# Two passes for three: one 512 column matmul for both parts of x in feed forwards, gates and down products

## The chip, the cores and the metric

One core of one Trainium2 chip runs the whole program. The metric is the device time of one execution in microseconds (us). Engines are named as in the profile: PE (TensorE) does matmuls into PSUM, PEld is its weight loads, DVE is VectorE, ACT is ScalarE, POOL is GpSimd, SP issues the DMAs of the weights.

## What is computed

Two transformer blocks of two layers each on 256 tokens of 1024 features, float32. Cut to what the change touches:

```python
def swiglu_ffn(h, w_up, w_down):                       # block one, twice a layer
    a, b = jnp.split(h @ w_up, 2, axis=-1)
    return (jax.nn.silu(a) * b) @ w_down
...
    x = x + 0.5 * swiglu_ffn(rmsnorm(x, ffn1_norm[l]), ffn1_w_up[l], ffn1_w_down[l])
    x = x + mixer(...)            # attention, conv; ends (g_attn * y_attn + g_conv * y_conv) @ w_out
    x = x + 0.5 * swiglu_ffn(rmsnorm(x, ffn2_norm[l]), ffn2_w_up[l], ffn2_w_down[l])
...
        up = dwconv_centred(h @ w_up[l], conv_w[l], conv_b[l])      # block two
        gate, val = up[..., :D_FF_2], up[..., D_FF_2:]
        x = x + (jax.nn.silu(gate) * val) @ w_down[l]
```

The feed forwards are 1024 -> 2 x 2816 -> 1024. The gates g_attn and g_conv are sigmoids of a 1024 -> 2 x 1024 product of the mixer's normed input.

## The kernel before

The residual stream x lies in SBUF as eight tiles of 128 features x 256 tokens. Each float32 product is made of float32r passes: an operand is split into a rounded part (h) and the rest (l), and W x = Wl xh + Wh xh + Wh xl. `mm3` (L326 to L332) issues these three passes, each 128x128 weights by 256 columns of tokens, into the same 256 columns of one PSUM bank. The weights are the stationary side.

The weights come as a stream of units of 128x1024 (some 128x768) values in the order of their use. `fetch` (L294) loads a unit into one of four raw buffers, `ahead` (L304) splits it: ScalarE copies the rounded part (wh, L312), VectorE subtracts (wl, L313). Splits run three units ahead of their use and loads six. Five buffers hold split units.

A feed forward (`ffn1` L467 in block one, `ffn2` L1141 in block two) has 22 up pairs and 8 down blocks. `up_pair` (L443) and `pair_half` (L432) take two units for 16 products of three passes: eight blocks of x, for the gate column block and the value column block side by side in one PSUM bank, 256 columns each. In block one `evac_up` (L474) then reads PSUM: VectorE t = pa * R (1/rms of the tokens, L476), ScalarE silu (L477), VectorE t * pb (L479), split into hh (ACT L338) and hl (DVE L339). 1/rms comes late: the products run on x * gain, the sum of squares is summed over partitions on TensorE after the first pair (`rms_cols`, L397) and spread to rows after the second (`rows`, L384), and the PSUM banks of the first pairs wait for it. In block two the first three pairs are treated so (L1159), and the later ones run on the normed x. There the evacuation is a conv of three taps (L1162 to L1164), silu and a product. `down` (L449) takes three units a block for 22 products into 256 columns of a bank. Its `evac` in block one is VectorE d = a * 0.5 * R (L497) and x + d (L498), in block two x + a (L1187). `operand` (L419) splits x * gain for the next stage into tiles xh and xl per block.

In block one's mixer the gates (`gate`, L806) are eight pairs like the up pairs. Their halves are laid between the heads of the attention by hand (L821 to L838). The result is multiplied by R on VectorE (L812, L813). The mixer's other products (`token_major`, L566) have x as the stationary side and the weights as 512 moving columns. Those of the conv (`conv_forward`, L661), of the attention's projection and of block two's mixer are outside the change but use its operands or its PSUM pool.

PSUM has two pools of four banks: `acc` (L246) gives a bank of 512 values from pool ps, `aux` (L249) one from pool px for scores, transposes and sums. The framework works out an order for each engine's instructions and the waits between engines from the program. A buffer is given out again when everything that used its tile is done. ScalarE's and VectorE's queues run in the order set then.

Of the kernel before, what the change touches and what calls it, by code (L numbers as in the profile page):

```python
# [27 lines left out]
P = 128  # L28
# [27 lines left out]
FIRST = {1: -5, 3: -4, 5: -3, 7: -2}  # L56
# buffers of the weight stream, and how many units its splits and its loads run ahead
# [70 lines left out]
def shape_tables():  # L128
# [29 lines left out]
    # cosines at the frequencies 0..128, sines at 1..127: the rest follows by symmetry  # L158
# [35 lines left out]
# ----------------------------------------------------------------------------------------------  # L194
class Kernel:
    def __init__(self, ctx, tc, aps):
# [14 lines left out]
        self.ps = pool("ps", 4, space=bass.MemoryType.PSUM)  # L211
# [19 lines left out]
        self.rawq, self.splq = {}, {}  # L231

# [13 lines left out]
    def acc(self, s="acc"):  # L246
        return self.ps.tile([P, 512], F32, tag="acc", name=self.nm(s))
# [69 lines left out]
    def unit(self, n):  # L317
        """Rounded part and rest of the next unit of the stream."""
# [7 lines left out]
    def mm3(self, out, wh, wl, xh, xl, start, stop, skip=False):  # L326
        """out += W^T x, stationary W"""
# [6 lines left out]
    def split(self, src, hi, lo, scale=None):  # L334
        """hi = rounded src * scale, lo = the rest"""
# [16 lines left out]
    def square_sum(self, blocks, scales=None):  # L352
        """Sum over blocks of (block * scale)^2, elementwise on [128, 256]"""
# [14 lines left out]
    def mean_rows(self, sacc, count, eps):  # L368
        """Every partition: mean over features + eps, [128, 256]"""
# [7 lines left out]
    def rows(self, r):  # L377
        """[128, 2] with tokens on partitions -> [128, 256], the same row on every partition"""
# [13 lines left out]
    def mean_cols(self, sacc, count, eps):  # L392
        """The same with tokens on partitions, [128, 2]"""
# [13 lines left out]
    def exp_table(self):  # L407
        """ScalarE's table of exp, ahead of the attention"""
# [3 lines left out]
    def combine_v(self, v1, vg):  # L412
        """(v1 * v2)^-1/2 with v2 = vg / v1 + eps, that is (vg + eps * v1)^-1/2"""
# [5 lines left out]
    def operand(self, srcs, gains, b0=0):  # L419
        hs, ls = [], []  # L420
        for b, x in enumerate(srcs, b0):
            h = self.op.tile([P, S], F32R, tag=f"xh{b}", name=self.nm("xh"))
            lo = self.op.tile([P, S], F32R, tag=f"xl{b}", name=self.nm("xl"))
            hv, lv = (h, lo) if len(x.shape) == 2 else (h.rearrange("p (j r) -> p j r", r=4),
                                                        lo.rearrange("p (j r) -> p j r", r=4))
            self.split(x, hv, lv, gains[b - b0])
            hs.append(h)
            ls.append(lo)
        return hs, ls

# [1 line left out]
    def pair_half(self, a, o, half):  # L432
        xh, xl = o
# [3 lines left out]
        for kk in range(4):  # L437
            k = half * 4 + kk
            for ab in range(2):
                self.mm3(a[:, ab * 256:(ab + 1) * 256], wh[:, kk, ab], wl[:, kk, ab], xh[k], xl[k],  # L440
                         k == 0 and ab == 0, k == KB - 1, skip=True)

    def up_pair(self, o):  # L443
        a = self.acc()
        for half in range(2):
            self.pair_half(a, o, half)
        return a[:, :256], a[:, 256:]

    def down(self, h, evac):  # L449
        for ob in range(KB):  # L450
            a = self.acc()
            for k0, k1 in DOWN:
                wh, wl = self.unit((k1 - k0) * P)
                for k in range(k0, k1):
                    c = slice((k - k0) * P, (k - k0 + 1) * P)
                    hh, hl = h[k]
# [3 lines left out]
    def h_slots(self):  # L460
        tiles = []
        for i in range(0, NF, 4):
            hi, lo = self.t4("hh", F32R), self.t4("hl", F32R)
            tiles += [(hi[:, j], lo[:, j]) for j in range(min(4, NF - i))]
        return tiles

    def ffn1(self, x, o, late, meanwhile=()):  # L467
        """x += 0.5 * swiglu(x_normed); the norm's 1/rms is applied to the products.  late: pieces to run after
        the first pairs, each with the result of the one before; the last one gives 1/rms"""
        nc = self.nc  # L470
        h = self.h_slots()
        R = None

        def evac_up(n, pa, pb):  # L474
            t = self.t1("t")
            nc.vector.tensor_tensor(t, pa, R, op=ALU.mult)  # L476
            nc.scalar.activation(t, t, AF.Silu)  # L477
            f = self.t1("f")
            nc.vector.tensor_tensor(f, t, pb, op=ALU.mult)  # L479
            self.split(f, *h[n])  # L480

        got, pend = None, []
        for n in range(NF):
            pend.append((n, *self.up_pair(o)))
# [820 lines left out]
```

## Time and profile before

| | |
|---|---|
| runs shown (3) | 1998.09, 2011.82, 2012.04 us; median 2011.82 |
| profiled execution, span from the first to the last instruction | 1994.0 us |
| mean granted clock of TensorE | 0.996 |
| TensorE matmuls | 14760, busy 1972.2 us |
| VectorE / ScalarE | busy 1393.5 / 1121.9 us |
| read from HBM | 335.65 MB, 169 GB/s over the span |

The profile gives the span of the profiled execution and no time of its own around it: of the runs shown the lowest is 4.1 us above the span, the median 17.8 us. A matmul's row shows when it started and how long until its last result was there. Since matmuls overlap, the distance between the starts of two is what one costs in a stream. PE's granted clock is given as a share of 2.4 GHz. A row of the timeline ends with the engine's idle time before the instruction and what ended it.

### The profile page before, as it was taken

The numbers are of one execution on the slowest core, as the hardware profiler recorded it, in microseconds if no ns is written. First come the engines' busy times: TensorE is split into PE (matmuls) and PEld (weight loads), VectorE is DVE, ScalarE is ACT, GpSimd is POOL, SyncE is SP. The second block draws the span as 40 slices with busy tenths as digits, with TensorE's granted clock in tenths as the row PEclk, the third lists the DMA queues.
The fourth block names the chain that finished last, engine by engine and source line by source line (L and its number), as shares of the span: only waits on it lengthen the run. The fifth ranks groups of instructions, "written<-read, shape, count | busy, mean of one in ns | idle before, by whom it ended". The sixth has DMA issues, their size and how long they took to land. (4 is left out here: it accounts for less than half of the span.)

```text
span 1994.0 us, 37071 instructions
## 1 busy us (share of the span) xinstructions
PE 1972.2 (99%) x14760; PEld 1881.0 (94%) x14760; DVE 1393.5 (70%) x2364; ACT 1121.9 (56%) x2133; POOL 113.9 (6%) x111
## 2 busy tenths in 40 slices
PE   8999999999999999999999999999999999999999
PEld 8999878899999999998788999999889999899999
DVE  6765687857666576656877567666768985669973
ACT  5544555647544455445556575444676764577662
POOL 1000022100000000000212000000100000100000
PEclk9999999999999999999999999999999999999999
DMA  8655655434555555556545245556334655524654
GB/s 263 194 179 182 218 169 167 154 96 159 180 182 183 176 177 191 175 185 212 177 165 165 79 154 180 183 178 182 122 127 149 199 177 179 181 96 161 203 179 125
DMA packets 97260, 339.09 MB, mean 170 GB/s; under 512 B 11430, under 2 KB 13574, under 8 KB 96960
## 3 DMA queue, kind: packets, MB, share of 16 engines
q1 hardware_dynamic: 93024, 326.63, 50.5%
q0 software_dynamic: 2944, 8.11, 1.7%
q8 instruction: 115, 1.88, 0.4%
q10 hardware_dynamic: 1120, 2.00, 0.3%
q14 instruction: 57, 0.47, 0.1%
HBM read 335.65 MB, written 1.05 MB: 169 GB/s over the span
## 5 line engine op out<-in xcount | busy, mean ns | idle before, releaser
L313 DVE TENSOR_TENSOR wl<-raw,wh 128x1024 fp32r<-128x1024 f32 (+1 forms) x634 | 758.7, 1199 | 351.2 <-ACT wh L312 346.2
L312 ACT ACTIVATE wh<-raw 128x1024 fp32r<-128x1024 f32 (+1 forms) x634 | 655.3, 1037 | 582.8 <-PE acc L332 273.1
L330 PE MATMUL acc<-xh,wl 128*128 128x256 f32 x1760 | 502.8, 286 | 4.6 <-DVE wl L313 4.5
L331 PE MATMUL acc<-xh,wh 128*128 128x256 f32 x1760 | 499.7, 284 | 0.0
L332 PE MATMUL acc<-xl,wh 128*128 128x256 f32 x1760 | 498.5, 283 | 0.0
L330 PEld LDWEIGHTS acc<-xh,wl 128*128 128x128 f32 x1760 | 338.1, 192 | 6.3 <-DVE wl L313 5.3
L331 PEld LDWEIGHTS acc<-xh,wh 128*128 128x128 f32 x1760 | 338.2, 192 | 0.8
L332 PEld LDWEIGHTS acc<-xl,wh 128*128 128x128 f32 x1760 | 338.0, 192 | 0.0
L330 PE MATMUL acc<-hh,wl 128*128 128x256 f32 x1056 | 298.8, 283 | 0.0
L331 PE MATMUL acc<-hh,wh 128*128 128x256 f32 x1056 | 298.8, 283 | 0.0
L332 PE MATMUL acc<-hl,wh 128*128 128x256 f32 x1056 | 298.8, 283 | 0.0
L330 PEld LDWEIGHTS acc<-hh,wl 128*128 128x128 f32 x1056 | 202.8, 192 | 0.0
L331 PEld LDWEIGHTS acc<-hh,wh 128*128 128x128 f32 x1056 | 202.8, 192 | 0.0
L332 PEld LDWEIGHTS acc<-hl,wh 128*128 128x128 f32 x1056 | 202.8, 192 | 0.0
L578 PE MATMUL acc<-wl,xh 128*128 128x512 f32 x480 | 189.7, 395 | 0.5 <-DVE wl L313 0.5
L579 PE MATMUL acc<-wh,xh 128*128 128x512 f32 x480 | 187.9, 392 | 0.0
L580 PE MATMUL acc<-wh,xl 128*128 128x512 f32 x480 | 187.8, 392 | 0.0
L330 PE MATMUL acc<-xn,wl 128*128 128x256 f32 x608 | 172.1, 283 | 0.0
L331 PE MATMUL acc<-xn,wh 128*128 128x256 f32 x608 | 172.1, 283 | 0.0
L332 PE MATMUL acc<-xn,wh 128*128 128x256 f32 x608 | 172.1, 283 | 0.0
L330 PEld LDWEIGHTS acc<-xn,wl 128*128 128x128 f32 x608 | 116.7, 192 | 0.0
L331 PEld LDWEIGHTS acc<-xn,wh 128*128 128x128 f32 x608 | 116.7, 192 | 0.0
(278 smaller groups left out, 3072.3 us busy)
## 6 DMA issues: line engine op xcount, KB each, us to landing
raw<-wts SPq DMA_DIRECT2D x576, 512.0 KB, 3.4
raw<-wts SPq DMA_DIRECT2D x48, 384.0 KB, 3.1
brow<-b_in POOLq DMA_DIRECT2D x26, 256.0 KB, 3.8
raw<-dft SPq DMA_DIRECT2D x4, 512.0 KB, 3.5
tab<-tab ACTq DMA_DIRECT2D x1, 1024.0 KB, 8.1
out<-x SPq DMA_DIRECT2D x8, 128.0 KB, 3.5
raw<-dft SPq DMA_DIRECT2D x2, 384.0 KB, 3.4
wraw<-conv_w POOLq DMA_DIRECT2D x6, 124.0 KB, 4.9
```

Of the source, the lines that this page charges most:

```text
L312: nc.scalar.activation(h[:, :n], r[:, :n], AF.Copy)
L313: nc.vector.tensor_tensor(lo[:, :n], r[:, :n], h[:, :n].bitcast(F32), op=ALU.subtract)
L330: mm(out, wl, xh, start=start, stop=False, **k)
L331: mm(out, wh, xh, start=False, stop=False, **k)
L332: mm(out, wh, xl, start=False, stop=stop, **k)
L578: mm(accs[t], xh[k][:, ts], wl[:, c], start=k == 0, stop=False)
L579: mm(accs[t], xh[k][:, ts], wh[:, c], start=False, stop=False)
L580: mm(accs[t], xl[k][:, ts], wh[:, c], start=False, stop=k == KB - 1)
```

## The change

The rounded part and the rest of each operand come to lie side by side in one tile of 2 x 256 columns (`operand`, and `pairs` for the hidden layer and the others). A new `mm2` issues two passes: Wh with all 512 columns, so that the left half of a bank collects Wh xh and the right half Wh xl, and Wl with xh into the right half. Whoever reads the result adds the halves. Up pairs and gates therefore take two banks each (gate columns in one, value columns in the other), and pool ps becomes two tiles of two banks. `acc` hands out the two banks of a tile one after the other. `mm2` is used in block one's up pairs, its gates, and in all down products. Block two's up pairs and all other products keep `mm3` and the single bank (`whole=True`). In block one `add_halves` reads PSUM with a ScalarE copy of the right halves and a VectorE add of the left ones, into SBUF, right after each pair and before R is there. Block two's down adds the two halves to x one after the other. In the conv two of three accumulators come from the other pool. The attention's transposed output is split in two pieces in place of one.

```diff
-        self.ps = pool("ps", 4, space=bass.MemoryType.PSUM)
+        self.ps = pool("ps", 2, space=bass.MemoryType.PSUM)
...
+    def acc2(self):
+        self.spare = None
+        return self.ps.tile([P, 2, 512], F32, tag="acc", name=self.nm("acc"))
+
+    def acc(self):
+        if self.spare is None:
+            t = self.ps.tile([P, 2, 512], F32, tag="acc", name=self.nm("acc"))
+            self.spare = t[:, 1]
+            return t[:, 0]
+        t, self.spare = self.spare, None
+        return t
...
+    def mm2(self, a, wh, wl, xp, start, stop):
+        mm = self.nc.tensor.matmul
+        mm(a, wh, xp, start=start, stop=False, skip_group_check=True)
+        mm(a[:, S:], wl, xp[:, 0], start=False, stop=stop, skip_group_check=True)
+
+    def add_halves(self, out, a):
+        self.nc.scalar.activation(out, a[..., S:], AF.Copy)
+        self.nc.vector.tensor_tensor(out, a[..., :S], out, op=ALU.add)
...
     def operand(self, srcs, gains, b0=0):
-            h = self.op.tile([P, S], F32R, tag=f"xh{b}", name=self.nm("xh"))
-            lo = self.op.tile([P, S], F32R, tag=f"xl{b}", name=self.nm("xl"))
...
+            t = self.op.tile([P, 2, S], F32R, tag=f"x{b}", name=self.nm("xo"))
...
+            for i in range(2):
+                if len(ab.shape) == 3:
+                    self.mm2(ab[:, i], wh[:, kk, i], wl[:, kk, i], o[k], k == 0, k == KB - 1)
+                else:
+                    self.mm3(ab[:, i * S:(i + 1) * S], wh[:, kk, i], wl[:, kk, i], o[k][:, 0], o[k][:, 1],
+                             k == 0 and i == 0, k == KB - 1, skip=True)
+
+    def up_pair(self, o, whole=False):
+        ab = self.acc() if whole else self.acc2()
...
-                    self.mm3(a[:, :256], wh[:, c], wl[:, c], hh, hl, k == 0, k == NF - 1)
-            evac(ob, a[:, :256])
+                    self.mm2(a, wh[:, c], wl[:, c], h[k], k == 0, k == NF - 1)
+            evac(ob, a)
...
-        def evac_up(n, pa, pb):
-            t = self.t1("t")
-            nc.vector.tensor_tensor(t, pa, R, op=ALU.mult)
+        def sums(ab):
+            t = self.t2("tu").rearrange("p (a c) -> p a c", a=2)
+            self.add_halves(t, ab)
+            return t
+
+        def evac_up(n, tu):
+            t, u = tu[:, 0], tu[:, 1]
+            nc.vector.tensor_tensor(t, t, R, op=ALU.mult)
             nc.scalar.activation(t, t, AF.Silu)
-            f = self.t1("f")
-            nc.vector.tensor_tensor(f, t, pb, op=ALU.mult)
-            self.split(f, *h[n])
+            nc.vector.tensor_tensor(t, t, u, op=ALU.mult)
+            self.split(t, h[n][:, 0], h[n][:, 1])
...
-            pend.append((n, *self.up_pair(o)))
+            pend.append((n, sums(self.up_pair(o))))
...
             t = self.t1("d")
-            nc.vector.scalar_tensor_tensor(t, a, 0.5, R, op0=ALU.mult, op1=ALU.mult)
+            self.add_halves(t, a)
+            nc.vector.scalar_tensor_tensor(t, t, 0.5, R, op0=ALU.mult, op1=ALU.mult)
...
-                    a = self.acc()
+                    a = self.acc() if i == 2 else self.aux("U")
...
             if half == 1:
-                nc.vector.tensor_tensor(blk(ga, n), a[:, :256], R, op=ALU.mult)
-                nc.vector.tensor_tensor(blk(gc, n), a[:, 256:], R, op=ALU.mult)
+                t = self.t2("gt").rearrange("p (a c) -> p a c", a=2)
+                self.add_halves(t, keep[-1])
+                nc.vector.tensor_tensor(blk(ga, n), t[:, 0], R, op=ALU.mult)
+                nc.vector.tensor_tensor(blk(gc, n), t[:, 1], R, op=ALU.mult)
...
-            ps = self.up_pair(early if n < EARLY else (hs, ls))
+            ps = self.up_pair(early if n < EARLY else xn, whole=True)
...
-        self.down(hsl, lambda ob, a: nc.vector.tensor_tensor(x[ob], x[ob], a, op=ALU.add))
+        def evac(ob, a):
+            for i in range(2):
+                nc.vector.tensor_tensor(x[ob], x[ob], a[:, i * S:(i + 1) * S], op=ALU.add)
+
+        self.down(hsl, evac)
```

## Rows read from the trace of the kernel before

**Rows 1.** The page's first part: busy us, share of the span, instructions.
```profile
PE 1972.2 (99%) x14760; PEld 1881.0 (94%) x14760; DVE 1393.5 (70%) x2364; ACT 1121.9 (56%) x2133; POOL 113.9 (6%) x111
```
**Rows 2.** Stretches: busy us (instructions) of PE, PEld, DVE, ACT, POOL; clock; DMA; GB/s.
```profile
100.00:200.00 100.00, 100.00 (x836) 100.00 (x835) 60.08 (x82) 45.43 (x61) 0.00 (x0) 1.00 0.58 181
1424.00:1432.00 8.00, 7.44 (x24) 5.92 (x23) 5.53 (x13) 3.77 (x5) 2.21 (x2) 0.57 0.29 87
1560.00:1640.00 80.00, 80.00 (x669) 80.00 (x668) 71.86 (x128) 54.05 (x89) 0.00 (x0) 1.00 0.59 194
```
**Rows 3.** Timeline of PE, up pairs of block one: start us, us, instruction.
```profile
103.15 0.28 PE L330 MATMUL acc<-xh,wl 128*128 128x256 f32 x1
...
103.51 0.28 PE L330 MATMUL acc<-xh,wl 128*128 128x256 f32 x1
```
**Rows 4.** Timeline of PE, the mixer's products of 512 columns.
```profile
252.99 0.39 PE L578 MATMUL acc<-wl,xh 128*128 128x512 f32 x1
...
253.67 0.39 PE L578 MATMUL acc<-wl,xh 128*128 128x512 f32 x1
```
**Rows 5.** Timeline of PE, passes of 128 columns in block two's Fourier part.
```profile
1470.60 0.27 PE L330 MATMUL acc<-Ah,wl 128*128 128x128 f32 x1
1470.71 0.28 PE L331 MATMUL acc<-Ah,wh 128*128 128x128 f32 x1
```
**Rows 6.** The page's costliest groups: xcount | busy us, mean ns | idle before.
```profile
L330 PE MATMUL acc<-xh,wl 128*128 128x256 f32 x1760 | 502.8, 286 | 4.6 <-DVE wl L313 4.5
...
L330 PE MATMUL acc<-hh,wl 128*128 128x256 f32 x1056 | 298.8, 283 | 0.0
```
**Rows 7.** Groups by line and form: copies and adds out of PSUM, and weight splits.
```profile
L312 ACT ACTIVATE wh<-raw 128x1024 fp32r<-128x1024 f32 x580 | 610.2, 1056 | 521.8 <-PE acc L332 235.5 <-issue 160.4 <-PE acc L580 81.8
...
L891 ACT ACTIVATE pT<-pt 128x512 f32<-128x512 f32 x48 | 28.4, 592 | 36.3 <-PE pt L889 36.3
...
L865 DVE TENSOR_TENSOR ga<-ga,acc 128x256 f32<-128x256 f32 x16 | 6.7, 420 | 8.9 <-PE acc L332 4.6 <-ACT ga L844 2.3 <-ACT gc L844 2.0
...
L386 ACT ACTIVATE R<-rows 128x256 f32<-128x256 f32 x14 | 5.2, 375 | 3.2 <-PE rows L384 3.1
...
L676 DVE TENSOR_TENSOR yr<-acc,What 128x512 f32<-128x512 f32 x2 | 1.4, 684 | 0.0
```
**Rows 8.** Timeline of DVE over one up pair of block one.
```profile
131.07 0.42 DVE L476 TENSOR_TENSOR t<-acc,R 128x256 f32<-128x256 f32 x1 [0.41 <-PE acc L332]
132.21 1.23 DVE L313 TENSOR_TENSOR wl<-raw,wh 128x1024 fp32r<-128x1024 f32 x1 [0.71 <-ACT wh L312]
133.35 0.41 DVE L479 TENSOR_TENSOR f<-t,acc 128x256 f32<-128x256 f32 x1
134.25 0.43 DVE L339 TENSOR_TENSOR hl<-f,hh 128x256 fp32r<-128x256 f32 x1 [0.48 <-ACT hh L338]
135.20 1.23 DVE L313 TENSOR_TENSOR wl<-raw,wh 128x1024 fp32r<-128x1024 f32 x1 [0.52 <-ACT wh L312]
136.83 0.42 DVE L476 TENSOR_TENSOR t<-acc,R 128x256 f32<-128x256 f32 x1 [0.41 <-PE acc L332]
```
**Rows 9.** Timelines of DVE and PE, from a down's end into the next feed forward.
```profile
712.59 0.42 DVE L497 SCALAR_TENSOR_TENSOR d<-acc,R 128x256 f32<-128x256 f32 x1
713.04 0.42 DVE L498 TENSOR_TENSOR x<-x,d 128x256 f32<-128x256 f32 x1
...
719.31 0.58 PE L397 MATMUL sumc<-ones,sacc 128*128 128x1 f32 x4 [0.41 <-DVE sacc L365]
```
**Rows 10.** Timeline of PE at the start of block two.
```profile
1422.90 0.58 PE L397 MATMUL sumc<-ones,sacc 128*128 128x1 f32 x4 [2.11 <-DVE sacc L365]
```
**Rows 11.** Timelines of PE (pair 4's first matmul) and DVE, block two's first feed forward.
```profile
1541.29 0.28 PE L330 MATMUL acc<-xn,wl 128*128 128x256 f32 x1
...
1539.54 0.42 DVE L1159 TENSOR_TENSOR pn<-acc,R 128x256 f32<-128x256 f32 x1
...
1542.62 0.42 DVE L1159 TENSOR_TENSOR pn<-acc,R 128x256 f32<-128x256 f32 x1
```

More of the change, by code (lines that the diff above doesn't have):

```diff
@@ L323, in unit, with pairs @@
         return h[:, :n], lo[:, :n]
+    def mm2(self, a, wh, wl, xp, start, stop):
[5 more added lines that the diff above has]
+        self.nc.vector.tensor_tensor(out, a[..., :S], out, op=ALU.add)
+    def pairs(self, n, s):
+        out = []
+        for i in range(0, n, 2):
+            t = self.t4(s, F32R)
+            out += [t[:, 2 * j:2 * j + 2] for j in range(min(2, n - i))]
+        return out
     def mm3(self, out, wh, wl, xh, xl, start, stop, skip=False):
@@ L419, in operand, with pair_half @@
     def operand(self, srcs, gains, b0=0):
-        hs, ls = [], []
+        ps = []
         for b, x in enumerate(srcs, b0):
-            h = self.op.tile([P, S], F32R, tag=f"xh{b}", name=self.nm("xh"))
-            lo = self.op.tile([P, S], F32R, tag=f"xl{b}", name=self.nm("xl"))
[L424 to L433, printed above, removed]
+            t = self.op.tile([P, 2, S], F32R, tag=f"x{b}", name=self.nm("xo"))
+            v = t if len(x.shape) == 2 else t.rearrange("p c (j r) -> p c j r", r=4)
+            self.split(x, v[:, 0], v[:, 1], gains[b - b0])
+            ps.append(t)
+        return ps
+    def pair_half(self, ab, o, half):
         wh, wl = self.unit(1024)
@@ L438, in pair_half @@
             k = half * 4 + kk
[L439 to L443, printed above, removed]
-        a = self.acc()
+            for i in range(2):
[6 more added lines that the diff above has]
+        ab = self.acc() if whole else self.acc2()
         for half in range(2):
-            self.pair_half(a, o, half)
-        return a[:, :256], a[:, 256:]
+            self.pair_half(ab, o, half)
+        return ab
     def down(self, h, evac):
@@ L718, in norm_rows @@
             stat["cR"] = self.rows(stat["cr"])
-        ch, cl = [], []
+        cp = []
         def norm_silu():
-            ch.extend(self.t4("ch", F32R) for _ in range(2))
-            cl.extend(self.t4("cl", F32R) for _ in range(2))
+            cp.extend(self.pairs(KB, "cp"))
             for b in range(KB):
@@ L728, in norm_silu @@
             for b in range(KB):
-                self.split(cb(b), ch[b // 4][:, b % 4], cl[b // 4][:, b % 4])
+                self.split(cb(b), cp[b][:, 0], cp[b][:, 1])
         after = {2: conv_forward, 4: lambda: conv_inverse(0)}
@@ L785, in pv @@
                 nc.tensor.matmul(Y[t][:, h * HD:(h + 1) * HD], pT[:, i * P:(i + 1) * P], w, start=i == 0, stop=i == 3)
-        yT = [self.t4("yTh", F32R), self.t4("yTl", F32R)]
+        yT = [self.t4("yT", F32R) for _ in range(2)]
         def finish(t, den):
@@ L853, in mixer @@
         sigmoids(ga, 0)
-        mh, ml = [self.t4("mh", F32R) for _ in range(2)], [self.t4("ml", F32R) for _ in range(2)]
+        mp = self.pairs(KB, "mp")
         for u in range(4):
@@ L876, in mixer @@
             nc.vector.tensor_tensor(blk(gc, ob), blk(gc, ob), blk(ga, ob), op=ALU.add)
-            self.split(blk(gc, ob), blk(mh, ob), blk(ml, ob))
+            self.split(blk(gc, ob), mp[ob][:, 0], mp[ob][:, 1])
         for ob in range(KB):
@@ L928, in mixer2 @@
         mm = nc.tensor.matmul
-        xh, xl = o
         acc = [self.acc(), self.acc()]
@@ L953, in mixer2 @@
         Ah, Al = self.t4("Ah", F32R), self.t4("Al", F32R)
-        yh = self.t4("yfh", F32R)
-        yl = self.t4("yfl", F32R)
+        yp = self.pairs(4, "yfp")
         yf = self.t4("yf")
@@ L1002, in f2 @@
                         mm(e, alt, A[:, fb, :130], start=False, stop=fb == 3 and A is Al, skip_group_check=True)
-                self.split(e[:1, :129], yh[:1, 2, :129], yl[:1, 2, :129])
-                self.split(e[:1, 127:0:-1], yh[:1, 2, 129:], yl[:1, 2, 129:])
-        mixed = [self.t4("mix", F32R) for _ in range(4)]
-        oph = [mixed[b // 4][:, b % 4] for b in range(KB)]
-        opl = [mixed[2 + b // 4][:, b % 4] for b in range(KB)]
+                self.split(e[:1, :129], yp[2][:1, 0, :129], yp[2][:1, 1, :129])
+                self.split(e[:1, 127:0:-1], yp[2][:1, 0, 129:], yp[2][:1, 1, 129:])
+        op = self.pairs(KB, "mix")
         def f3(ob):
@@ L1031, in proj @@
                 c = slice(((ob % 2) * 4 + k) * P, ((ob % 2) * 4 + k + 1) * P)
-                kk = half * 4 + k
-                self.mm3(out, wh[:, c], wl[:, c], oph[kk], opl[kk], k == 0 and ob % 2 == 0, k == 3, skip=True)
+                self.mm3(out, wh[:, c], wl[:, c], op[half * 4 + k][:, 0], op[half * 4 + k][:, 1], k == 0 and ob % 2 == 0, k == 3, skip=True)
             if half == 1:
@@ L1147, in ffn2 @@
         R = None
-        xn = [self.t4("xn", F32R) for _ in range(4)]
-        hs = [xn[b // 4][:, b % 4] for b in range(KB)]
-        ls = [xn[2 + b // 4][:, b % 4] for b in range(KB)]
-        hsl = self.h_slots()
+        xn = self.pairs(KB, "xn")
+        hsl = self.pairs(NF, "hp")
         def evac_up(n, ps):
             ts = []
-            for ab, p in enumerate(ps):
+            for ab in range(2):
+                p = ps[:, ab * S:(ab + 1) * S]
                 i = ab * NF + n
@@ L1208, in run @@
                 self.ahead(-2)
-            for dst, part in zip(o, self.operand(x[b:b + 1], [self.v(0, "ffn1_norm", b)], b)):
-                dst += part
+            o += self.operand(x[b:b + 1], [self.v(0, "ffn1_norm", b)], b)
         late = (lambda _: self.square_sum(x), self.rms_cols, self.rows)
```

61 lines of the change are left out of this document (26 added, 35 removed).

## Prediction

> **What bounds the kernel now.** I read the page's first part first: TensorE is busy for 99% of the span, VectorE 70%, ScalarE 56% [rows 1]. "Busy" says little for an engine whose matmuls overlap, so next come the busy times by stretch: in the feed forwards TensorE has no idle time at full clock, VectorE is busy 60 us in 100 in block one's (up and down mixed) and 72 in 80 in block two's up products, and the DMA engines about 0.58 [rows 2]. Then the timeline of TensorE, for the distance from one matmul's start to the next. In a feed forward three passes of 256 columns start at 103.15, 103.27, 103.39 and the next product at 103.51: 0.36 us for three, 120 ns a pass [rows 3]. In the mixer's products passes of 512 columns take 0.68 us for three, 226.7 ns each [rows 4]. The 256 columns between the two cost 106.7 ns, which is 2.4 GHz; so each pass carries 120 - 106.7 = 13.3 ns besides its columns, whichever its width. That is the quantity on which the change turns: columns stay, passes go. (A mean of 283 or 392 ns in the groups is latency, and their difference must not be taken for a pitch.)
>
> **The change part by part.** Before, a product is Wl xh, Wh xh, Wh xl: three passes of 256 columns, 360.0 ns. After, Wh meets xh and xl in one pass of 512 and Wl meets xh in one of 256: 226.7 + 120.0 = 346.7 ns. Saved: 13.3 ns a product.
>
> How many: the group with x's two halves counts 1760 [rows 6]. By the code 4 feed forwards x 22 pairs x 16 products are 1408 of them, 2 layers x 8 gates x 16 are 256; the other 96 are block two's first three up pairs (2 x 3 x 16), which keep three passes. The group with h counts 1056 = 6 feed forwards x 176, all changed. So 1408 + 256 + 1056 = 2720 products, and 2720 x 13.3 ns = **36.3 us** off TensorE's stream. Nothing else bounds those stretches, so all of it would come off the end if no wait appeared.
>
> A pass of 128 columns also starts only every 0.11 us [rows 5]: a floor which the column count doesn't explain, presumably the weight load beside it. A 256 pass lies just above the floor and a 512 pass far above, so a 512 pass followed by a 256 pass hides both loads as now. Were the floor to add rather than hide, rows 4 would show more than 226.7.
>
> The Trainium skill ("TensorE: Matmul & The Clock Gate", section "Back-to-back issue gap") gives N/2.4 + 2.5 ns for a pass. By that rule the merged pass would save 2.5 ns a product, 6.8 us in all, and the change would be worth nothing after its costs; rows 3 and 4 show 13.3 at both widths, so I go by the rows and keep the rule as a rival.
>
> What is added, and where it lies:
> - Block one's up pairs: one ScalarE copy of 128x512 out of PSUM (592 ns) and one VectorE add of 128x512 (684 ns) [rows 7] for each of 88 pairs. A pair now lasts 16 x 346.7 ns = 5.55 us. VectorE's work for one is 3.71 us now (t, f, hl and two splits of weights [rows 8]) and becomes 4.40 us, 79%; ScalarE's rises by 0.59 us. It hides behind TensorE: in block two's up products VectorE runs at 90% and TensorE doesn't wait [rows 2]. If that cover were gone it would cost up to 88 x 0.68 us (a rival below).
> - Block one's down and every gate: copy and add of 128x256 in the first (375 ns and 420 ns [rows 7]), of 128x512 in the second. Down has 7.6 us for each block of outputs, with some 4.7 us of VectorE's work: nothing, except at its last block. There the chain last matmul, d, x [rows 9] gets 0.80 us longer (0.38 + 0.42). TensorE waits for what follows at two places: for the sum of squares at 719.3 [rows 9] and at 1422.9 [rows 10]. I add 0.80 us at each; at the first also 0.21 us because the up pair ahead of the wait is shorter (16 x 13.3 ns), and 0.68 us because the first pair's add now falls into the busy stretch of VectorE before the rows of 1/rms. Together 2.5 us (from 0 to 4). The clock is at its lower level for part of 1424 to 1432 (granted 0.57 [rows 2], that is 1.2 GHz for most of it) after the idle time before; a longer wait may move that by some microseconds either way, and I count nothing for it.
> - Gates: the copies and adds, 8 a layer, go into the attention, where VectorE has gaps except around the conv's norm. From 0 to 8 x 0.68 = 5.5 us a layer; near the lower end, because a gate's sum is not needed until the attention is over: 1.0 us for both layers.
> - PSUM: four single banks become two tiles of two. A tile comes free when both banks have been read. In block two's up products pair 4 takes the bank of pair 0, whose last read is over at 1540.0, before pair 4 starts at 1541.29. Now it needs pair 1's as well, whose last read starts at 1542.62 and takes 0.42 [rows 11]: 1543.04 - 1541.29 = 1.75 us of wait, in each of two layers 3.5 us. From 0 (if VectorE's order changes) to about 8 (if pair 6 waits too).
> - The conv's products take two of three accumulators from the other PSUM pool and the mixer's accumulators come in pairs: 0.5 us (0 to 2).
> - Block two's down reads PSUM with two adds for one, 0.42 us more; only the last of each layer shows, 0.8 us together. Start: the weights arrive no faster for a faster TensorE, 0.4 us.
> - The DMA engines must bring 3 to 4% more a second, from a share of 0.58 [rows 2]: nothing. The relayout of x, h, ch and m into pairs issues the same splits: nothing.
>
> Sum: 36.3 - 2.5 - 1.0 - 3.5 - 0.5 - 0.8 - 0.4 = **27.6 us** saved. The profiled execution's span goes from 1994.0 to 1966.4 us. The runs shown lie at 1998.1, 2011.8 and 2012.0, so 4 to 18 us lie around the span or differ from run to run; I take the same 27.6 us off the median: 2011.8 - 27.6 = **1984 us** (1.4%). A measurement of this kernel tells about 1% from no change, that is 20 us.
>
> **The rivals.**
> 1. The 13.3 ns is no cost of a pass but of something that the merged pass keeps (the floor of rows 5 points that way, the equal excess at 256 and 512 columns speaks against). With 2.5 ns saved a product, 6.8 us less the 8.7 us of costs: 2 us slower, 2014 us, no change. By the Trainium skill's rule quoted above this is what would come out.
> 2. Two PSUM tiles are too few at the head of every feed forward, where the splits of x and the squares fill ScalarE and VectorE. In steady state the release comes at worst 4.8 us after a pair's end (behind one split of 1.06 on ScalarE [rows 7], then 0.59, two splits of 1.22 on VectorE, then 0.68), within the 5.55 us that the next pair lasts; with eight squares in front (8 x 0.38, as the 128x256 copy of rows 7) it is 2.2 us over. Four feed forwards x 2.2 us more: 27.6 - 9 = 18.6 us saved, 1993 us, within 1%. For it: pair 4's wait above is of this kind. Against: the sum is read at once and no longer waits for 1/rms.
> 3. Slower: VectorE takes over in block one's up products. Its queue is in order, and now idles 0.41 + 0.71 + 0.48 + 0.52 us a pair and between instructions [rows 8]: 5.76 - 3.71 = 2.05 us. If these waits for ScalarE stayed while the work grows to 4.40, a pair would take 6.45 us, 88 x (6.45 - 5.76) = 61 us lost. Gates and down keep (256 + 1056) x 13.3 = 17.5 us and the 8.7 us of costs stay: 2011.8 + 61 - 17.5 + 8.7 = 2064 us. It decides from a VectorE cycle of 5.55 us on (gain gone at 5.76). For it: a new handover from ScalarE to VectorE in each pair. Against: the waits end with TensorE's or ScalarE's pace, not with VectorE's, the splits have three units in hand to fill them, and 90% busy is seen to work [rows 2].
>
> **How the numbers follow.** Forecast 0.72 (savings from 17 to 36 us, nearly all of it over 1%), rival 1 0.07, rival 2 0.13, rival 3 0.08. Faster by over 1%: 0.74 (the forecast's, and the part of rival 2 with little wait); within 1%: 0.18; slower by over 1%: 0.08. The range reaches down to no cost at all and a run like the lowest before (2011.8 - 36.3 less some 10 of run to run spread, 1966), and up past rival 2 to half of the gain lost with a slow run, 2006.
>
> **What would show each step.** Right: in block one's up products a wide pass starts 226 to 227 ns before the narrow one and that 120 ns before the next wide one; TensorE has some 12040 matmuls (14760 - 2720); a pair takes 5.55 us, a block of down 7.63 us; VectorE is near 79% there with TensorE at 100%; at block two's pair 4 a wait on VectorE's reads of about 1.7 us; waits for the sum of squares 0.8 to 1.0 us longer. Wrong: a wide pass of over 230 ns or a narrow one of over 125; TensorE waiting for an accumulator in each pair, or for wl; a pair's period over 5.7 us.

## The result and the profile after

The changed kernel takes 2032.8 us (median of 7 runs, 2022.0 to 2037.8), the kernel before beside it 2009.4 (7 runs, 1994.1 to 2012.0). The ratio is 1.0136 [1.0098, 1.0174]: **slower by 1.4%**, where 1.4% faster was forecast. The profiled executions have spans of 2020.2 and 1994.0 us, at mean granted clocks of 0.989 and 0.996.

The page's first part, after, beside [rows 1]:

```profile
PE 1971.4 (98%) x12040; PEld 1742.0 (86%) x12040; DVE 1473.9 (73%) x2520; ACT 1180.5 (58%) x2273; POOL 113.6 (6%) x111
```

The 2720 matmuls are gone (14760 to 12040), and yet TensorE's busy time has not moved. So the products were merged as told, and the time went elsewhere. The stretches say where to look. After (columns as in [rows 2], with three more stretches of block two):

```profile
100.00:200.00 100.00, 99.71 (x560) 85.85 (x559) 67.27 (x97) 50.81 (x75) 1.07 (x2) 1.00 0.59 190
...
1460.00:1480.00 20.00, 19.02 (x126) 16.87 (x126) 10.57 (x36) 10.78 (x33) 0.00 (x0) 0.84 0.21 70
1480.00:1500.00 20.00, 20.00 (x133) 18.20 (x133) 8.27 (x27) 13.47 (x35) 1.80 (x3) 0.84 0.10 33
1560.00:1640.00 80.00, 77.67 (x646) 77.33 (x646) 69.02 (x122) 51.10 (x85) 0.00 (x0) 1.00 0.52 180
1760.00:1780.00 20.00, 19.15 (x123) 16.44 (x122) 10.62 (x37) 10.50 (x34) 0.00 (x0) 0.83 0.23 79
```

The kernel before, same view, stretches that [rows 2] lacks:

```profile
1460.00:1480.00 20.00, 19.93 (x144) 17.65 (x144) 10.96 (x37) 14.55 (x46) 0.00 (x0) 0.94 0.24 80
1480.00:1500.00 20.00, 20.00 (x157) 18.70 (x157) 13.67 (x43) 14.10 (x35) 1.80 (x3) 1.00 0.26 81
...
1760.00:1780.00 20.00, 20.00 (x156) 18.63 (x155) 12.34 (x39) 15.18 (x41) 1.26 (x2) 1.00 0.25 83
```

Two things differ. TensorE now has idle time in block two's up products, which keep their three passes (77.67 of 80, before 80.00). And in block two's mixers the granted clock is 0.83 to 0.84, before 0.94 to 1.00. Added up over all stretches of 20 us (twice what is missing to 1.00, times the length), TensorE ran at its lower level of 1.2 GHz for 45 us after, for 17 us before. What that costs is seen in one product of the changed kernel (timeline of TensorE; the clock of 1456 to 1462 is 0.50):

```profile
1460.66 0.41 PE L1001 MATMUL acc<-wl,uh 128*128 128x256 f32 x1
1460.88 0.41 PE L999 MATMUL acc<-wh,uh 128*128 128x256 f32 x1
1461.09 0.41 PE L1000 MATMUL acc<-wh,ul 128*128 128x256 f32 x1
```

A pass of 256 columns starts every 0.21 us there, at the upper level every 0.12 [rows 3].

Next the waits of TensorE, which is the view that names the cause. After (waiting instruction, what ended the wait: us in total, times, longest):

```profile
PE acc L363 <- DVE cv L1189: 4.1, 3, 1.8
...
PE acc L607 <- DVE z L775: 3.5, 2, 1.8
PE acc L363 <- DVE pn L1184: 3.3, 2, 1.6
PE acc L343 <- DVE cv L1189: 3.1, 2, 1.5
PE sumc L430 <- DVE sacc L398: 2.4, 1, 2.4
PE acc L363 <- DVE fs L1065: 1.8, 2, 0.9
...
PE Y L1114 <- ACT pT L922: 1.7, 2, 0.9
...
PE acc L363 <- DVE gt L349: 1.5, 2, 0.7
...
PE acc L363 <- DVE ga L896: 1.5, 2, 0.7
...
PE acc L343 <- DVE x L1215: 1.1, 1, 1.1
```

The whole list adds up to 44.6 us, that of before to 17.5. Of these only the sum of squares has an entry before, and but for it and Y all are alike: the waiting product (acc) opens an accumulator, and the wait ends with VectorE's read of another (cv, pn, z, fs, gt, ga and x read one). Two of them in the timelines, each time VectorE's read and then TensorE's first product into the bank:

```profile
315.54 0.75 DVE L775 SCALAR_TENSOR_TENSOR z<-acc,rc,brow 128x512 f32<-128x512 f32 x1
...
316.34 0.50 PE L607 MATMUL acc<-wl,xo 128*128 128x512 f32 x1 [1.77 <-DVE z L775]
...
1548.58 0.42 DVE L1184 TENSOR_TENSOR pn<-acc,R 128x256 f32<-128x256 f32 x1
...
1549.05 0.39 PE L363 MATMUL acc<-xn,wl 128*128 128x256 f32 x1 [1.64 <-DVE pn L1184]
```

The second is pair 4 of block two, which answers to [rows 11]; the first is in block one's mixer, where 0.5 us was allowed for all such places.

Last the passes themselves, answering to [rows 3]. After, timeline of TensorE in the first and in the second feed forward:

```profile
102.98 0.40 PE L343 MATMUL acc<-xo,wh 128*128 128x512 f32 x1
...
104.05 0.40 PE L343 MATMUL acc<-xo,wh 128*128 128x512 f32 x1
...
559.71 0.39 PE L343 MATMUL acc<-xo,wh 128*128 128x512 f32 x1
...
561.10 0.39 PE L343 MATMUL acc<-xo,wh 128*128 128x512 f32 x1
```

From 102.98 to 104.05 are three products, from 559.71 to 561.10 four. Over the whole stretches the distances repeat as 350, 361, 349 ns in the one (353.3 a product) and as 350, 343 or 347, 347, 346 in the other (346.7, the forecast). So only part of the products save the 13.3 ns; the others save 6.7. The forecast's two parts, 226.7 and 120 ns, are in neither: the narrow pass starts 231 to 233 ns after the wide one in the quicker rhythm and 233 to 241 in the slower, and the next wide one 112 to 118 and 113 to 120 ns after that.

### The profile page after: what moved, and what is told of

Read it like the earlier page. It is cut to its first block, busy times and chain, and to the rows that moved or that the text cites. A ratio compares the mean times of both kernels' runs of the same rounds, so it can differ in the third digit from the quotient of the medians.

```text
span 2020.2 us, 31942 instructions
## 1 busy us (share of the span) xinstructions
PE 1971.4 (98%) x12040; PEld 1742.0 (86%) x12040; DVE 1473.9 (73%) x2520; ACT 1180.5 (58%) x2273; POOL 113.6 (6%) x111
## 4 chain that ended last, share of the span: by engine, by line
PE 69%; issue 16%; DVE 8%; ACT 3%; POOL 3%; DMA 1%; POOLq 0%; DVEq 0%; SPq 0%; ACTq 0%
PE acc L343 23%; PE acc L344 12%; PE acc L363 7%; PE acc L365 6%; PE acc L364 6%; DVE wl L327 3%; POOL rs L568 2%; PE acc L607 2%; PE acc L608 2%; PE acc L609 2%; PE Y L813 1%; ACT wh L326 1%; PE pt L920 1%; PE s L1095 1%; PE s L797 1%
## 5 line engine op out<-in xcount | busy, mean ns | idle before, releaser
L343 PE MATMUL acc<-xo,wh 128*128 128x512 f32 x1664 | 591.2, 399 | 4.3 <-ACT wh L326 3.8
L344 PE MATMUL acc<-xo,wl 128*128 128x256 f32 x1664 | 466.7, 281 | 0.5 <-DVE wl L327 0.5
L343 PEld LDWEIGHTS acc<-xo,wh 128*128 128x128 f32 x1664 | 313.6, 189 | 77.6 <-ACT wh L326 4.0
L343 PE MATMUL acc<-hp,wh 128*128 128x512 f32 x1056 | 370.7, 395 | 4.1 <-DVE cv L1189 3.1
L344 PEld LDWEIGHTS acc<-xo,wl 128*128 128x128 f32 x1664 | 314.8, 189 | 2.3 <-DVE wl L327 1.5
L344 PE MATMUL acc<-hp,wl 128*128 128x256 f32 x1056 | 296.4, 282 | 0.2
L343 PEld LDWEIGHTS acc<-hp,wh 128*128 128x128 f32 x1056 | 197.8, 188 | 50.4 <-issue 5.0
L344 PEld LDWEIGHTS acc<-hp,wl 128*128 128x128 f32 x1056 | 199.3, 189 | 5.7 <-DVE wl L327 5.2
L607 PE MATMUL acc<-wl,xo 128*128 128x512 f32 x480 | 189.0, 394 | 5.2 <-DVE z L775 3.5
L609 PE MATMUL acc<-wh,xo 128*128 128x512 f32 x480 | 187.1, 390 | 0.0
L608 PE MATMUL acc<-wh,xo 128*128 128x512 f32 x480 | 187.0, 390 | 0.0
L608 PEld LDWEIGHTS acc<-wh,xo 128*128 128x128 f32 x480 | 90.2, 188 | 17.5
```

The source lines that it names most:

```text
L343: mm(a, wh, xp, start=start, stop=False, skip_group_check=True)
L344: mm(a[:, S:], wl, xp[:, 0], start=False, stop=stop, skip_group_check=True)
L607: mm(accs[t], o[k][:, 0, ts], wl[:, c], start=k == 0, stop=False)
L608: mm(accs[t], o[k][:, 0, ts], wh[:, c], start=False, stop=False)
L609: mm(accs[t], o[k][:, 1, ts], wh[:, c], start=False, stop=k == KB - 1)
```

## Experiments

**Single banks (1), and the kernel before with paired ones (2).** The theory: the two-bank tiles make the waits, the waits lower the clock. Kernel 1 is the changed kernel with four single banks (each bank's halves are then added by themselves):

```diff
-        self.ps = pool("ps", 2, space=bass.MemoryType.PSUM)
+        self.ps = pool("ps", 4, space=bass.MemoryType.PSUM)
...
     def acc2(self):
-        return self.ps.tile([P, 2, 512], F32, tag="acc", name=self.nm("acc"))
+        return [self.acc(), self.acc()]
...
     def acc(self):
+        return self.ps.tile([P, 512], F32, tag="acc", name=self.nm("acc"))
...
-            self.add_halves(t, ab)
+            for i in range(2):
+                self.add_halves(t[:, i], ab[i])
```

> The changed kernel with four single accumulator banks again in place of two tiles of two: the up products of block one and its gates take two banks of their own, and the halves of each bank are added by themselves (two copies of 256 columns on ScalarE and two additions on VectorE for each pair in place of one of each). The wide pass and the narrow pass stay. Theory A (the pairing of the banks makes the waits in the mixers and in block two, and these waits lower the clock): those waits go back to what they were (conv inverse, attention projection, pairs 4 and 6, head of the down products each under 0.5 us), the clock is at its lower level for about 17 us and not 44, and the time falls from 2033 to about 1990 (1980 to 2000), below the kernel before. Rival B (the two-pass stream of TensorE is itself slower than its 347 ns, with its stalls): 2025 to 2035, the waits gone without the time going. Rival C (the extra work of ScalarE and VectorE): 2035 to 2060, since this kernel adds 96 instructions to each of them and more.

Measured: 1970.4 us, 0.987 [0.9826, 0.9915] of the kernel before, and 10 us under the range that the theory gave. Its list of waits adds up to 18.8 us; all those shown above but the one for the sum of squares are gone:

```profile
PE tr L585 <- DVE z L573: 4.8, 4, 1.9
PE sumc L422 <- DVE sacc L390: 2.8, 2, 2.4
PE acc L335 <- ACT wh L318: 1.8, 2, 1.5
PE acc L600 <- DVE wl L319: 1.4, 2, 1.0
```

Kernel 2 is the mirror: the kernel before, `ps` with two buffers and the changed kernel's `acc`; three passes, no additions.

> The kernel before with one edit: its accumulators come two and two out of two tiles of two banks, as in the changed kernel; all products stay three passes of 256 columns, and nothing is added on reading. Theory A: the waits for a tile of which the other half is still read show up here as in the changed kernel (2 us in the conv's inverse, 1 to 2 us at pairs 4 and 6 and at the head of the down products of block two), some 15 us of them and some 10 us of clock: 2009 becomes 2025 to 2040. Rivals B and C: 2009 within 5 us, since neither the passes nor the additions are there.

Measured: 2063.5 us, 1.0339 [1.0285, 1.0392]. Pairing alone costs 64 us, more than expected, and shows the changed kernel's waits:

```profile
PE acc L337 <- DVE wl L320: 9.2, 19, 3.2
PE acc L337 <- DVE cv L1171: 7.3, 5, 1.8
...
PE acc L585 <- DVE z L754: 3.5, 2, 1.8
PE acc L337 <- DVE pn L1166: 3.3, 2, 1.6
```

The 19 waits for weights (wl, in the kernel before two) are a second effect of the pairing. The listing of TensorE's queue in the changed kernel shows it (number, line, output<-operands):

```
760 L344 MATMUL acc_244_1464<-hp_34_179,wl_247_1468 128x256
761 L343 MATMUL acc_265_1599<-hp_24_169,wh_259_1556 128x512 [waits Activation_49]
...
776 L344 MATMUL acc_265_1599<-hp_27_172,wl_260_1557 128x256
777 L343 MATMUL acc_244_1464<-hp_24_169,wh_249_1489 128x512 [waits DVE_49]
```

In the down products the framework puts eight products (in block two some four) of the output block after next (tile acc_265, weights 259 and 260) ahead of the next block, which lies in the second bank of the tile acc_244 that is just being read, though the bank itself is free. These early products need weights that have hardly been split. The changed kernel has 20 such places, kernel 1 and the kernel before none; that the framework orders so because it takes the tile as one is inferred from this. Such a place in the changed kernel's timeline of TensorE:

```profile
147.50 0.39 PE L343 MATMUL acc<-hp,wh 128*128 128x512 f32 x1
147.89 0.39 PE L344 MATMUL acc<-hp,wl 128*128 128x256 f32 x1
148.11 0.40 PE L343 MATMUL acc<-hp,wh 128*128 128x512 f32 x1
```

The product takes 0.61 us where others take 0.35. TensorE is not idle by the list of waits, since a row lasts until its last result is there. The distances between the starts show some 0.27 us more at 16 of the 20 places, 4.3 us in all.

**Three passes in the changed kernel (3), in single banks (5).** In both the 2720 products become three passes into the same two halves:

```diff
-        mm(a, wh, xp, start=start, stop=False, skip_group_check=True)
-        mm(a[:, S:], wl, xp[:, 0], start=False, stop=stop, skip_group_check=True)
+        mm(a[:, S:], wl, xp[:, 0], start=start, stop=False, skip_group_check=True)
+        mm(a[:, :S], wh, xp[:, 0], start=False, stop=False, skip_group_check=True)
+        mm(a[:, S:], wh, xp[:, 1], start=False, stop=stop, skip_group_check=True)
```

> The changed kernel with its 2720 two-pass products as three passes of 256 columns into the same two halves of a bank; the layout of the operands, the paired banks and the additions on reading stay. It measures the two-pass product alone: by the steady pitches (360 ns for three passes against 347 in one half of the stages and 353 in the other) it should cost 2720 x 7 to 13 ns, 18 to 36 us, over the changed kernel where the product is on the path: 2050 to 2068 by theory A. By rival B (the stream of two passes brings stalls and clock with it) it comes out at 2020 to 2035, no slower than the changed kernel.

> The kernel with single banks (the first experiment) with its 2720 products as three passes of 256 columns into the same two halves of a bank. With it all four corners of passes and banks are there. The theory now: the two edits add up, the two-pass product saves 2720 x 7 to 13 ns wherever the banks are single or paired, so this kernel takes 1970 + 27 (19 to 36) = 1997, as much as the kernel before (1990 to 2005); the additions on reading and the layout of the operands cost nothing. Rival C (the additions cost, and single banks only hide it): 2005 to 2020, above the kernel before.

Measured: 2059.0 us, 1.03 [1.0243, 1.0356], and 1993.8 us, 0.9943 [0.9922, 0.9963]. Both are as the theory has it; the additions and the layout cost nothing that these runs show.

Each run also has its mean granted clock, and time follows it: in 61 runs the kernel before goes from 1990 us at 0.999 to 2012 at 0.986 (slope of the fit 1.7 us for 0.001). So the clock can be taken out: span times mean clock, averaged over a kernel's runs (good to some 3 us, since not all time at the lower level is TensorE's).

| kernel | median us | mean clock | span x clock |
|---|---|---|---|
| before: 3 passes, single | 2009.4 | 0.992 | 1985 |
| 5: 3 passes, single, additions | 1993.8 | 0.997 | 1985 |
| 1: 2 passes, single | 1970.4 | 0.995 | 1961 |
| 2: 3 passes, paired | 2063.5 | 0.984 | 2033 |
| 3: 3 passes, paired, additions | 2059.0 | 0.986 | 2028 |
| after: 2 passes, paired | 2032.8 | 0.986 | 2000 |

(Medians of before differ between the runs' sets, 1999 to 2009 us; the ratios are each to its own.) Read down the last column: two passes save 24 us with single banks and 28 with paired ones; pairing costs 39 us with two passes, 43 to 48 with three; the additions cost 0. On top comes the clock, 0.984 to 0.986 in these three paired kernels: 0.006 less than before's 0.992 is some 11 us. Kernel 5's 0.997 against the 0.992 of before has no cause that these runs show: the same passes, banks and time at equal clock, and nothing is put into its waits.

**The narrow pass first (4).** The two `mm` lines of the changed kernel change places.

> The changed kernel with the narrow pass (256 columns, the rest of the weights) ahead of the wide one (512 columns) in each product; nothing else. Rival B: if the 353 ns of the first feed forward of each layer, against 347 ns in the second, come from which pass follows which, or from the wait of the narrow pass on VectorE's part of the split, this changes it: either all stages at 347 (about 10 us less, 2023) or all at 353 (about 10 us more, 2043). Theory A: no change beyond 5 us, since the waits lie elsewhere.

Measured: 2026.9 us, 1.014 [1.0098, 1.0182], as the changed kernel; both rhythms are still there. The order of the passes is not what sets them. (Its mean clock is 0.992 and span x clock 2010: at equal clock it is 10 us slower, which the theory did not expect and no run explains, and it had the better clock with the same pairing. So pairing makes a low clock likelier, not certain.)

**Kicks (8).** One product of ones, 64 columns, ahead of every fourth up pair of kernel 1 (5 in each of block one's four feed forwards; the next product overwrites its result).

```diff
+        if kick:
+            self.nc.tensor.matmul(ab[0][:, :64], self.ones, self.ones[:, :64], start=True, stop=True)
```

> The kernel with single banks with one product of ones of 64 columns ahead of every fourth pair of up products in block one's feed forwards (20 in all, some 5 us in all), overwritten by the first product. It asks why a two-pass product takes 353 ns in one feed forward and 347 in the other. If the rhythm is set by the phase with which a run of products starts, a product of another length changes it: the feed forwards then show both means, changing at these places. If it is set by the tiles (addresses, banks), each feed forward keeps its mean.

One run, 1980.3 us. The same stretch of the second feed forward (the same tiles), kernel 1 and then this kernel:

```profile
620.00:700.00 80.00, 80.00 (x464) 69.97 (x463) 55.48 (x82) 41.56 (x65) 0.00 (x0) 1.00 0.61 189
```

```profile
620.00:700.00 80.00, 80.00 (x456) 69.44 (x455) 54.29 (x82) 41.14 (x65) 0.00 (x0) 1.00 0.56 183
```

464 matmuls in 80 us are 80 x 2 / 464, 345 ns a product; 456 are 351 (counts at a stretch's ends make some 1 ns). The change comes at the product of ones itself (two passes, L471). Timeline of TensorE at the first one in the second feed forward:

```profile
536.71 0.39 PE L335 MATMUL acc<-xo,wh 128*128 128x512 f32 x1
...
538.10 0.33 PE L471 MATMUL acc<-ones 128*128 128x64 f32 x2
...
538.68 0.40 PE L335 MATMUL acc<-xo,wh 128*128 128x512 f32 x1
...
539.74 0.40 PE L335 MATMUL acc<-xo,wh 128*128 128x512 f32 x1
```

Four products in 1.39 us before it, three in 1.06 us soon after. In kernel 1 some 1240 products run at 346.7 and 1310 at 353.3, here 205 and 2290. So the start of a run of products sets its rhythm, not the tiles. The rhythm does not change at every product of ones, as expected: after nearly all of them it is the slower one. What in TensorE has these two rhythms stays open.

**Filled waits (6).** The changed kernel, with products of ones in two places of block two's mixer:

```diff
+            for _ in range(7 if hf == 0 else 0):
+                mm(a[:, :P], self.ones, self.ones, start=True, stop=True)
...
+            for _ in range(5 if (t, pr) == (0, 1) else 0):
+                mm(Y[t][:, c:c + HD], self.ones, self.ones[:, :HD], start=True, stop=True)
```

> The changed kernel with paired banks, and in each layer's mixer of block two seven products of ones of 128 columns ahead of the first Fourier product and five of 64 columns ahead of the second pair of heads' values, written where the next product overwrites them; they stand where TensorE waited 1 to 3 us. The theory of the clock (the new waits lower it in these stretches, some 27 us more at the lower level, 13 us of time): with the waits filled the lower level shrinks from 45 us to under 25 us and the time falls by 5 to 12 us, to 2021 to 2028, though TensorE does more. The rival (the clock falls for another reason, the waits alone cost): the time stays or rises by 2 to 4 us, 2033 to 2037, and the lower level stays at about 45 us.

Measured: 2016.6 us (10 runs), 1.0052 [1.0028, 1.0075] where the changed kernel had 1.0136. That is less than the 2021 to 2028 that the theory gave. Span x clock rises by 4 us to 2004, the mean clock from 0.986 to 0.994. The profiled execution, the longest of the ten (2035.9 us), had 65 us at the lower level and not under 25, so the lower level comes less often, and not never; the reading rests on the runs.

**Paired in one block only (9, 10).** The PSUM pool is closed and opened anew between the blocks.

> Two-pass products as in the changed kernel; the accumulators are paired (two tiles of two banks) in block one and single in block two. Theory: the cost of the pairing is a sum of places, and by the stage ends of the two profiles (the first product that reads block one's result: 1420.1 us in the changed kernel, 1399.4 us with single banks) block one has some 20 us of it and block two, with the clock, some 35 us. So this kernel takes 1970 + 20 = 1990 (1982 to 2000). A rival: pairing anywhere brings the lower clock, 2010 and more.

> The same with the accumulators single in block one and paired in block two. Theory: 1970 + 35 = 2005 (1995 to 2015), with the waits at the second pair of heads' values, at the output projection, at pairs 4 and 6 and at the head of the down products as in the changed kernel, and over 30 us at the lower clock in the mixers of block two. If the lower clock of the changed kernel comes from block one's waits, it is missing here and the time is 1985 to 1990.

Measured: 2001.7 us, 0.9994 [0.9966, 1.0023], and 2005.4 us, 1.0011 [0.9985, 1.0037]. Span x clock: 1985 and 1982, so 24 us of the pairing's cost lie in block one and 21 in block two (39 when both are paired). Kernel 9 is above its 1982 to 2000: block one's part was forecast at 20 us and is 24 at equal clock, 31 with the clock. Kernel 10 came as forecast (35 us with the clock). The waits sit where the pairs are. Groups of kernel 9, then of kernel 10:

```profile
L372 PE MATMUL acc<-xn,wl 128*128 128x256 f32 x608 | 172.1, 283 | 0.0
L372 PE MATMUL acc<-yT,wl 128*128 128x256 f32 x64 | 19.8, 316 | 4.3 <-DVE gt L358 4.3
```

```profile
L372 PE MATMUL acc<-xn,wl 128*128 128x256 f32 x608 | 172.5, 284 | 7.4 <-DVE cv L1200 4.1 <-DVE pn L1195 3.3
...
L372 PE MATMUL acc<-yT,wl 128*128 128x256 f32 x64 | 18.1, 283 | 0.0
```

For the clock neither text was right: kernel 9 has a mean of 0.991 though its block two is that of kernel 1 (0.995), and in its profiled execution it lost the clock in block two's first mixer, not where its own waits are. Kernel 10 has 0.990, and in its profiled execution 20 us at the lower level in block two's mixers, where over 30 were expected.

**Two passes in block two's up products too (7).** Single banks, and 704 more products in two passes, halves added ahead of the conv taps:

```diff
-            ps = self.up_pair(early if n < EARLY else xn, whole=True)
+            ps = self.t2("tu")
+            pb = self.up_pair(early if n < EARLY else xn)
+            for i in range(2):
+                self.add_halves(ps[:, i * S:(i + 1) * S], pb[i])
```

> The kernel with single banks, and block two's 704 up products in two passes as well, with the halves added (a copy on ScalarE and an addition on VectorE for each bank) ahead of the conv taps. If the product is what counts: 704 x 7 to 13 ns, 5 to 9 us less than 1970: 1961 to 1965. If VectorE becomes the bound there (it has the conv's taps as well, and the additions are 2 x 0.42 us more for each pair): a pair would take longer than the 10.4 us of its products, 1975 to 1990.

Measured: 1978.3 us, 0.9871 [0.9832, 0.991]: nothing over kernel 1. Its stretch of up products:

```profile
1560.00:1640.00 80.00, 79.79 (x453) 68.96 (x452) 75.97 (x154) 60.75 (x115) 0.00 (x0) 1.00 0.54 183
```

VectorE is at 75.97 of 80 and TensorE begins to wait for the weights' second part (wl): these products' passes take 4 us less, their waits 5 us more. So VectorE eats the gain: 19 pairs take 110.3 and 109.5 us in the two layers, 109.3 in kernel 1. The time lies in the second expectation's range, but its reason holds only in part: at equal clock kernel 7 takes 1963 us against 1961, and a pair's products take 5.6 us, not the 10.4 that it names.

**The wait filled in kernel 1 (11) and in the kernel before (12).** The first of the two edits of kernel 6, in each.

> The kernel with single banks, with seven products of ones of 128 columns ahead of the first Fourier product of each layer of block two, where TensorE waits 1 to 2.4 us in that kernel's profile. Each run of that kernel lies on a line of its time against its mean granted clock (1967 us at 1.000, 1985 us at 0.987). If the wait is what lowers the clock in its slower runs, the runs gather at 0.997 and above: 1965 to 1970 in all of them, median 1968. If not, the median stays at 1970 to 1975 with the same spread of clocks.

> The kernel before with the same seven products of ones ahead of the first Fourier product of each layer of block two; nothing of the change. It tells what of the filled single-bank kernel's gain (1969 against 2003 us) is the filling. Theory: the runs of the kernel before lie on a line against their mean granted clock too (1990 us at 0.999, 2012 at 0.986; the mean is 0.9916), and the filling gathers them near 0.997: 1993 to 1997 us, a ratio of 0.995 to 0.998, so that some 8 us of the 34 are the clock's and 26 the two passes'. The rival (the filling does nothing by itself): 2003 to 2006 with clocks between 0.986 and 0.999 as before.

Measured: 1968.6 us (1967.7 to 1970.1), 0.9813 [0.9778, 0.9848], all clocks 0.997 or 0.998; and 1995.5 us (1992.5 to 1998.6), 0.9962 [0.9931, 0.9993], mean clock 0.996. Kernel 11 beats the kernel before by 1.9% and the changed one by some 3%. The filling alone is worth 0.4% in the kernel before; the rest is the two passes.

## Why the prediction was wrong

The forecast was 1984 us (1966 to 2006); 2032.8 was measured. It went to none of its cases: slower, but not by its slower rival. By its own steps:

- **The products.** 2720, as counted (14760 - 12040). The term was 36.3 us; the runs show 24 to 28, that is 9 to 10 ns a product and not 13.3. The pitches of [rows 3] and [rows 4] were each right, and their sum holds in one of two rhythms only; a stream of one width didn't show the other. Mis-sized by some 10 us. That the quicker rhythm is 346.7, as forecast, is in part luck, since its two parts are not 226.7 and 120; a wide pass of over 230 ns was named as a sign of being wrong.
- **PSUM: the step that failed.** "Four single banks become two tiles of two" was given 3.5 us (0 to 8), and 0.5 us for the mixers' accumulators. Pair 4's wait came as worked out (1.75 forecast, 1.64 measured), and with pair 6 the waits of those up products are 7.4 us, inside the 0 to 8. But they were some of many places: the head of block two's down products, its output projection, the product behind the conv's inverse (3.5 us alone), the attention's projection, and the reordered down products. Together 39 us at equal clock (kernel 1 to the changed kernel). The two profiled executions differ by 33 us at equal clock (1997 and 1965); their lists of waits make 26 of it (44.6 - 18.8), the reordered down products 4, and the rest was not traced to a place (the 39 are means of the runs). The prediction worked out one place and gave 0.5 us to the mixers and nothing to the down products, where its own rule, "A tile comes free when both banks have been read", holds at every accumulator.
- **The clock.** "I count nothing for it": 0.992 to 0.986 in the mean, 11 us. Waits in block two's mixer have a part in it: with products of ones in them the mean clock is 0.994 in place of 0.986 (kernel 6), 0.998 in place of 0.995 (kernel 11, four runs) and 0.996 in place of 0.992 (kernel 12, all ten runs at 0.995 to 0.997, where 20 of 61 of the kernel before reach 0.995), with the same work otherwise. They are not shown to be all of it: kernel 5 has 0.997 with nothing filled, and kernel 4 has 0.992 with the pairing. Which wait tips it in a given run stays open (kernels 4 and 9).
- **What held.** The additions cost nothing (kernel 5 against before: 1985 and 1985). The gates' sums (1.0 us) and the tails (2.5 us) are at most that: with single banks none of their waits is left but the sum of squares, 2.4 us where [rows 10] has 2.11. The sum without the PSUM and accumulator terms, 36.3 - 2.5 - 1.0 - 0.8 - 0.4 = 31.6 us, is to be set beside kernel 1's 24 at equal clock; what is missing is the products' term.
- **The rivals.** Rival 1 (2.5 ns saved a product) would leave 6.8 us; 24 to 28 were measured. The Trainium skill ("TensorE: Matmul & The Clock Gate", section "Back-to-back issue gap") gives the rule quoted in the prediction for a matmul by itself and says that a stream with weight loads goes by other figures, so it was no rule for this stream. Rival 2 had the right cause, too few tiles, at the wrong places: up pairs of block one hardly wait (99.71 of 100 busy). Rival 3 fell: VectorE is at 67 of 100 there, with up and down mixed (44.3 of 60 from 80 to 140 us, up pairs alone: 74% where 79 was forecast), and TensorE sets the pace; what it describes begins in kernel 7, in block two.

The balance at equal clock, from the kernel before: -24 for the passes and +39 for the pairing (by way of kernel 1), or 0 for the additions, +43 for the pairing and -28 for the passes (by way of kernels 5 and 3). Both make the +15 of 2000 - 1985, as they must, since each is a chain of differences. With 11 for the clock that is 26; the medians differ by 23.4, and the ratio of 1.0136 is 27.

The Trainium skill ("Perfetto Trace Analysis", section "Matmuls") says that independent groups of matmuls should go round through different PSUM banks, so that reading one overlaps the next. The runs agree, with 39 to 48 us for handing out the same four banks two by two. The Trainium skill ("TensorE: Matmul & The Clock Gate", section "A second HAM failure mode: psum-queue depth-cycling") tells of another kernel, where short idle times between groups of matmuls make the clock swing between its levels; mean clocks of 0.984 to 0.986 in three kernels with all banks paired agree, against 0.992 to 0.997 with single ones; the 0.992 of kernel 4 doesn't.

## What to carry to other kernels

A buffer's size is also its granularity of release: before merging two accumulators into one tile, go through every user of that pool, not the one that the change is about, and ask which read now holds up which write. An engine at 99% has no slack for this, and its waits can cost twice, where they take its clock along. When many runs scatter, put each against its granted clock before comparing: here that took 23 us of scatter down to 7 (kernel before, 61 runs).

## What the runs showed of the hardware

- A stream of alternating 512 and 256 column passes has two rhythms, 346.7 and 353.3 ns a pair of passes; it keeps the one with which it began until something interrupts it. One product of 64 columns turned the quicker into the slower at 538.10 us of kernel 8.
- A mixture of short waits, 0.9 to 2.4 us each, in a kernel busy for 98% of its span, goes with a mean clock lower by 0.6%, 11 us; seven products of ones in one such wait raised it by 0.003 and 0.004 in two kernels with single banks, at no cost in time (1962.6 and 1985.8 us at equal clock, 1961.2 and 1985.1 without them). That the waits alone do it is not shown: two kernels of one time at equal clock, before and kernel 5, differ by 0.005 with none of them filled.
